# A quarter of the weight tiles' remainders on GpSimd in the mixing stages of a two-layer hybrid backbone

## The chip, the core and the metric

The kernel runs on one core of a Trainium2 chip. The metric is the device time of one launch in microseconds (us). Three runs of the kernel before gave a median of 2957.7 us. The engines are named as in the profile: PE is the matrix engine's matmul row (TensorE), PEld its weight load, DVE is VectorE, ACT is ScalarE, POOL is GpSimd, SP issues the DMAs. Each engine works through its own list of instructions in the order in which they stand, and waits at the first whose inputs or buffers are not ready.

## What is computed

Two layers over 256 latent and 256 context tokens of width 1024, in float32. Cut to what matters here:

```python
def layer(x, s, l):                       # x latent tokens, s context tokens, 256 of each
    x, s = ffn_sublayer(x, ...), ffn_sublayer(s, ...)        # SwiGLU, D_FF = 2816
    hx, hs = modulate(rms_norm(x)), modulate(rms_norm(s))
    cols = h @ w_in                                          # the wide projection of both streams
    ret = retention(cols[...])                               # 8 heads
    att = window_context_attention(cols[...])                # 8 heads
    rw = rwkv7(cols[...])                                    # 8 heads, forward and backward scan
    x = x + gate * ((g_ret * (ret @ w_ret) + g_att * (att @ w_att) + g_rw * (rw @ w_rwkv)) @ w_out)
    x = ffn_sublayer(x, ...)
```

In the second layer the mixing stage works out the latent tokens' results alone.

## The kernel before

**Products.** Every weight product is made of three matmuls in a rounded float32 format (`mm3`, L185 to L188): a value is split into a rounded part and the remainder. Lines 186, 187 and 188 multiply rounded weight by rounded activation, rounded weight by the activation's remainder, and the weight's remainder by the rounded activation. Where tokens are the output rows (`tokens`), the weight stands on the other side, and line 187 then reads the weight's remainder.

**Weight tiles.** `Weights.get` fetches the weights in the order of a plan, four 128x128 blocks (one tile of 128x512) at a time: SP issues a DMA into `raw` (8 buffers), ACT rounds it into `whi` (L114, 4 buffers), and DVE subtracts to give the remainder `wlo` (L115, 3 buffers). Three stages of a layer each have a `Weights` object: the first feed-forward, the mixing stage, the second feed-forward. The mixing stages' object is made with a fifth argument True, which is kept as `s.pool` and used nowhere.

**The mixing stage.** It runs over the words of `ORDER[l]`: `c` makes the columns of a pair of rwkv heads, `A` and `C` (`rw_front`, `rw_prep`) prepare its first and second 256 tokens, `B` and `D` (`rw_back`) finish them, `P` and `H` are retention, `kv`, `q`, `t` attention, `G` gates. At the end `branches` and `mix_out` multiply by the branch and output weights.

**The recurrence.** `rw_prep` ends in a triangular solve: a loop of 31 steps with two dependent GpSimd operations in each, a product (L999) and a sum (L1000), 62 operations in all. Its input `acc` comes by DMA through DRAM, and its result goes to `td` in DRAM and comes back as `z`. `rw_merge` then copies `z` on ACT (L1017), transposes it on DVE (L1014, L1018), and PE starts on it at L1026. There are 16 of these solves, for four pairs, two halves and two layers; below they are counted 0 to 15 in the order in which they run. Besides them POOL does only a few small copies (L921, L922, L934, L937) and 8 subtractions of 128x512 (L851).

**Order.** The order of instructions on every engine is not written out by hand. A scheduler at build time takes the program's order as priority and lets an instruction go when its own timing says that it is ready. A changed line so moves instructions on all engines.

Of the kernel before, what the change touches and what calls it, by code (L numbers as in the profile page):

```python
# [7 lines left out]
F32 = mybir.dt.float32  # L8
# [80 lines left out]
class Weights:  # L89
# [14 lines left out]
    def get(s, t, n=1):  # L104
        p = t // PB
        if p not in s.cur:
            nc = s.nc
            cols = min(PB, s.n - p * PB) * 128
            raw = s.mk([128, PB * 128], "raw", 8)[:, :cols]
            hi = s.mk([128, PB * 128], "whi", 4, F32R)[:, :cols]  # L110
            lo = s.mk([128, PB * 128], "wlo", 3, F32R)[:, :cols]
            o = p * PB * 16384
            s.last = nc.sync.dma_start(out=raw, in_=s.ap[o:o + 128 * cols].rearrange("(p c) -> p c", p=128)).ins
            nc.scalar.copy(hi, raw)  # L114
            nc.vector.tensor_sub(lo, raw, hi.bitcast(F32))  # L115
            s.cur = {q: v for q, v in s.cur.items() if q == p - 1}
            s.cur[p] = (hi, lo)
        hi, lo = s.cur[p]
        c = (t % PB) * 128
        return hi[:, c:c + 128 * n], lo[:, c:c + 128 * n]  # L120
# [1232 lines left out]
```

## Time and profile before

| | |
|---|---|
| median of three runs | 2957.7 us (2949.77 to 2957.78) |
| the profiled execution | 2949.03 us, span 2947.2 us |
| mean granted clock of PE | 0.965 of full speed |
| busy: PE, DVE, ACT, POOL | 96%, 68%, 43%, 13% of the span |
| mixing stages, both layers | 405 to 1310 us and 2060 to 2750 us of the span |

Busy shares are averages over the span. A busy PE is not a PE at its peak: at half the granted clock the same matmul takes longer and counts as busy.

### The profile page before, as it was taken

Reading aid. Unit: us, or ns where it says so; the run is one execution under the profiler, and the core shown is the slowest. Engines: PE = TensorE matmul, PEld = TensorE weight load, DVE = VectorE, ACT = ScalarE, POOL = GpSimd, SP = SyncE. Lnnn points to the kernel's source line nnn. Section 1 sums busy time; section 2 is a strip of 40 time slices with the busy share of each in tenths; the row PEclk is TensorE's granted clock in tenths of the full one; section 3 lists DMA queues with packets and bytes.
Section 4 is the critical chain, followed back from the end, with each engine's and each line's share of the span. In section 5 each row is a group of like instructions: output and inputs, shape, how many; then the busy total and the mean of one; then the engine's idle time right before and its main releaser. Section 6 shows DMA issues by size and latency. Waiting matters only on the chain.

```text
span 2947.2 us, 47745 instructions
## 1 busy us (share of the span) xinstructions
PE 2821.4 (96%) x17081; PEld 2413.6 (82%) x17081; DVE 1991.8 (68%) x4561; ACT 1261.4 (43%) x2776; POOL 372.5 (13%) x1068
## 2 busy tenths in 40 slices
PE   8999999899999999899999999999989899989999
PEld 7888888777887787688888888888878788878999
DVE  7977668776685765467756567455777677667655
ACT  3322245545445544333222332223556565655544
POOL 0000000622032201000000000000033344330000
PEclk9999999878999999899999999999999899999999
DMA  7655544222332145434635345344333244246554
GB/s 267 232 189 184 163 122 131 83 67 58 118 101 86 53 129 188 136 111 155 202 129 160 122 132 170 127 147 138 116 112 110 65 120 120 69 128 198 164 182 158
DMA packets 259726, 400.98 MB, mean 136 GB/s; under 512 B 78752, under 2 KB 96288, under 8 KB 259488
## 3 DMA queue, kind: packets, MB, share of 16 engines
q1 hardware_dynamic: 259488, 397.93, 43.1%
q8 instruction: 134, 2.20, 0.3%
q14 instruction: 104, 0.85, 0.1%
HBM read 368.33 MB, written 25.82 MB: 134 GB/s over the span
## 4 chain that ended last, share of the span: by engine, by line
PE 79%; POOL 7%; DVE 5%; DMA 4%; issue 2%; ACT 2%; SPq 1%; POOLq 0%; DVEq 0%; ACTq 0%
PE ps_mm L186 21%; PE ps_mm L187 20%; PE ps_mm L188 20%; POOL cst L1000 3%; POOL cst L999 3%; PE ps_rf L971 2%; PE ps_mm L364 1%; PE ps_po L774 1%; PE ps_rx L1075 1%; PE ps_rx L1068 1%; PE ps_rx L364 1%; PE ps_po L559 1%; DMA z<-td 1%; DVE wlo L115 1%; DMA td<-cst 1%
## 5 line engine op out<-in xcount | busy, mean ns | idle before, releaser
L186 PE MATMUL ps_mm<-hall,whi 128*128 128x512 f32 (+1 forms) x2320 | 843.2, 364 | 6.4 <-ACT kv L711 2.7
L114 ACT CAST whi<-raw 128x512 fp32r<-128x512 f32 x954 | 568.4, 617 | 655.1 <-PE ps_mm L187 429.7
L188 PE MATMUL ps_mm<-hall,wlo 128*128 128x512 f32 (+1 forms) x2320 | 839.7, 363 | 1.0 <-DVE wlo L115 1.0
L187 PE MATMUL ps_mm<-hall,whi 128*128 128x512 f32 (+1 forms) x2320 | 839.0, 362 | 0.0
L115 DVE TENSOR_TENSOR wlo<-raw,whi 128x512 fp32r<-128x512 f32 x954 | 645.8, 689 | 230.0 <-issue 106.8
L186 PEld LDWEIGHTS ps_mm<-hall,whi 128*128 128x128 f32 x2320 | 441.0, 190 | 78.5 <-ACT kv L711 3.1
L188 PEld LDWEIGHTS ps_mm<-hall,wlo 128*128 128x128 f32 x2320 | 439.9, 190 | 72.1 <-DVE wlo L115 2.4
L187 PEld LDWEIGHTS ps_mm<-hall,whi 128*128 128x128 f32 x2320 | 440.6, 190 | 70.5 <-issue 0.3
L186 PE MATMUL ps_mm<-hid,whi 128*128 128x512 f32 (+1 forms) x737 | 260.6, 354 | 0.0
L187 PE MATMUL ps_mm<-hid,whi 128*128 128x512 f32 (+1 forms) x737 | 259.9, 354 | 0.0
L188 PE MATMUL ps_mm<-hid,wlo 128*128 128x512 f32 (+1 forms) x737 | 257.4, 354 | 0.0
L999 POOL TENSOR_TENSOR cst<-acc,cst 128x60 f32<-128x60 f32 (+24 forms) x496 | 171.9, 347 | 599.7 <-DMA acc<-ad__10854 71.0
L851 POOL TENSOR_TENSOR ll<-lora,lh 128x512 fp32r<-128x512 f32 x8 | 10.2, 1278 | 1380.9 <-DMA raw<-w1b 949.7
L1000 POOL TENSOR_TENSOR cst<-cst 128x60 f32<-128x60 f32 (+24 forms) x496 | 172.7, 348 | 37.8
L236 DVE SCALAR_TENSOR_TENSOR ft<-m,cd 128x1024 bf16<-128x1024 f32 x136 | 162.8, 1219 | 6.0 <-DMA m<-ada 6.0
L237 DVE SCALAR_TENSOR_TENSOR m<-m,cd 128x1024 f32<-128x1024 f32 x136 | 165.3, 1220 | 0.7
L373 DVE SCALAR_TENSOR_TENSOR x<-ps_mm,cst,x 128x256 f32<-128x256 f32 x136 | 61.0, 480 | 146.6 <-PE ps_mm L188 146.3
L187 PEld LDWEIGHTS ps_mm<-hid,whi 128*128 128x128 f32 x737 | 139.1, 189 | 19.5
L186 PEld LDWEIGHTS ps_mm<-hid,whi 128*128 128x128 f32 x737 | 139.0, 189 | 19.5
L188 PEld LDWEIGHTS ps_mm<-hid,wlo 128*128 128x128 f32 x737 | 138.5, 189 | 19.4
L401 DVE TENSOR_TENSOR ft<-ft,ps_mm 128x512 f32<-128x512 f32 (+1 forms) x80 | 49.6, 620 | 126.1 <-PE ps_mm L188 120.7
L210 ACT CAST hid<-ft 128x512 fp32r<-128x512 f32 (+1 forms) x88 | 49.9, 568 | 192.5 <-DVE ft L401 192.4
(338 smaller groups left out, 4560.8 us busy)
## 6 DMA issues: line engine op xcount, KB each, us to landing
m<-ada SPq DMA_DIRECT2D x136, 512.0 KB, 4.3
raw<-w0b SPq DMA_DIRECT2D x214, 256.0 KB, 2.9
raw<-w1b SPq DMA_DIRECT2D x211, 256.0 KB, 3.0
raw<-w0a SPq DMA_DIRECT2D x132, 256.0 KB, 3.0
raw<-w0c SPq DMA_DIRECT2D x132, 256.0 KB, 3.1
raw<-w1a SPq DMA_DIRECT2D x132, 256.0 KB, 3.0
raw<-w1c SPq DMA_DIRECT2D x132, 256.0 KB, 3.9
gd<-ft SPq DMA_DIRECT2D x24, 256.0 KB, 2.6
```

The source lines that it names most:

```text
L114: nc.scalar.copy(hi, raw)
L115: nc.vector.tensor_sub(lo, raw, hi.bitcast(F32))
L186: PE.matmul(o, w[0], h[0], start=start, stop=False)
L187: PE.matmul(o, w[0], h[1], start=False, stop=False)
L188: PE.matmul(o, w[1], h[0], start=False, stop=stop)
L236: V.scalar_tensor_tensor(junk, raw, 1.0, st["cond"][0], ALU.mult, ALU.mult, accum_out=md[:, kt, 0:1])
L237: V.scalar_tensor_tensor(raw, raw, 1.0, st["cond"][1], ALU.mult, ALU.mult, accum_out=md[:, kt, 1:2])
L364: PE.matmul(o[:, p], w[k, j][q], hl(H[k], p)[0], start=(k == 0 and q == 0 and p.start == c.start), stop=False)
L373: V.scalar_tensor_tensor(xs[n][:, CS[s]], o[:, CS[s]], gate[:, n, s:s + 1], xs[n][:, CS[s]], ALU.mult, ALU.add)
L971: PE.matmul(ov[:, q, 0:n], kb[d][hs, q].rearrange("p a t -> p (a t)"), ar[d][hs, q].rearrange("p a t -> p (a t)")[:, 0:n], start=True, sto ...
L999: G.tensor_tensor(w, acc[j // 16][:, j % 16, j + 1:32].unsqueeze(1).to_broadcast([128, m, n]), tt[:, 0:m, j:j + 1].to_broadcast([128, m, n ...
L1000: G.tensor_tensor(tt[:, 0:m, j + 1:32], tt[:, 0:m, j + 1:32], w, ALU.add)
```

## The change

One line. In the mixing stages every fourth weight tile (those with number 3, 7, 11, ... of the plan) has its remainder taken on GpSimd:

```diff
@@ -112,7 +112,7 @@
             o = p * PB * 16384
             s.last = nc.sync.dma_start(out=raw, in_=s.ap[o:o + 128 * cols].rearrange("(p c) -> p c", p=128)).ins
             nc.scalar.copy(hi, raw)
-            nc.vector.tensor_sub(lo, raw, hi.bitcast(F32))
+            (nc.gpsimd if s.pool and p % 4 == 3 else nc.vector).tensor_sub(lo, raw, hi.bitcast(F32))
             s.cur = {q: v for q, v in s.cur.items() if q == p - 1}
             s.cur[p] = (hi, lo)
         hi, lo = s.cur[p]
```

104 of the 954 remainders change engine (some tiles are fetched twice, by `tokens`). The set of instructions is otherwise the same, but their order is not: 26 of the 104 now stand inside a recurrence. In recurrence 13 (second layer, its input is `acc_23514`) POOL's list read, before:

```order
L999 TENSOR_TENSOR cst_63<-acc_23514,cst_63 128x69
L1000 TENSOR_TENSOR cst_63<-cst_63 128x3x23
L999 TENSOR_TENSOR cst_63<-acc_23514,cst_63 128x66
L1000 TENSOR_TENSOR cst_63<-cst_63 128x3x22
L999 TENSOR_TENSOR cst_63<-acc_23514,cst_63 128x63
```

and now:

```order
L999 TENSOR_TENSOR cst_63<-acc_23514,cst_63 128x69
L1000 TENSOR_TENSOR cst_63<-cst_63 128x3x23
L999 TENSOR_TENSOR cst_63<-acc_23514,cst_63 128x66
L115 TENSOR_TENSOR wlo_24534<-raw_24532,whi_24533 128x512
L1000 TENSOR_TENSOR cst_63<-cst_63 128x3x22
L999 TENSOR_TENSOR cst_63<-acc_23514,cst_63 128x63
```

A tile's subtraction stands between two dependent steps; a second one (`wlo_25020`) follows 18 operations later.

The copies of `z` of the same recurrence, on ACT in the second layer. Before, they stood right behind the first two activations of the next half's preparation (L908, L909):

```order
L908 ACTIVATE rt_25091<-ps_rf_25093,cst_63 128x256
L909 ACTIVATE rt_25092<-ps_rf_25093,cst_63 128x256
L1017 COPY tg_19027<-z_24814 32x8x32 x2
L772 COPY aT_24336<-ps_ap_24335 128x512
L1077 COPY ve_24611<-ps_rx_24640 64x128
```

Now they stand further back, behind L939 of that preparation, and `aT_24336` has gone ahead of them:

```order
L918 ACTIVATE rt_25117<-rt_25108 128x512
L919 ACTIVATE rt_25118<-rt_25108 128x512
L765 ACTIVATE ae_24352,cst_63<-ps_sc_24351,cst_63 128x512
L939 ACTIVATE rt_25131<-rt_25092,cst_63 128x512
L1017 COPY tg_19027<-z_24814 32x8x32
L777 ACTIVATE cst_63<-cst_63 128x4
L1077 COPY ve_24611<-ps_rx_24662 64x128
```

DVE's transposes of that `z` moved back by as much.

The third place is recurrence 4 (first layer, its input is `acc_7793`), on POOL. Before, no tile stood there. Now one stands behind the first 17 operations of the recurrence:

```order
L1000 TENSOR_TENSOR cst_63<-cst_63 128x2x24
L999 TENSOR_TENSOR cst_63<-acc_7793,cst_63 128x69
L115 TENSOR_TENSOR wlo_8526<-raw_8524,whi_8525 128x512
L1000 TENSOR_TENSOR cst_63<-cst_63 128x3x23
L999 TENSOR_TENSOR cst_63<-acc_7793,cst_63 128x66
```

The tile `wlo_8526` has to wait for that recurrence's input and steps, and PE for the tile.

## Rows read from the trace of the kernel before

**Rows 1.** The page: busy time by engine, and the chain of waits by engine.

```profile
PE 2821.4 (96%) x17081; PEld 2413.6 (82%) x17081; DVE 1991.8 (68%) x4561; ACT 1261.4 (43%) x2776; POOL 372.5 (13%) x1068
...
PE 79%; POOL 7%; DVE 5%; DMA 4%; issue 2%; ACT 2%; SPq 1%; POOLq 0%; DVEq 0%; ACTq 0%
```

**Rows 2.** Busy time by stretch: span, PE, PEld, DVE, ACT, POOL, clock, DMA.

```profile
405.00:1130.00 725.00, 691.38 (x4467) 582.20 (x4466) 501.37 (x1338) 368.11 (x906) 175.20 (x532) 0.94 0.31 91
1130.00:1310.00 180.00, 167.65 (x854) 133.01 (x853) 104.93 (x214) 66.62 (x130) 0.00 (x0) 0.95 0.50 167
...
2060.00:2640.00 580.00, 535.20 (x4087) 469.74 (x4085) 423.27 (x1121) 333.73 (x817) 197.11 (x532) 0.95 0.37 105
2640.00:2750.00 110.00, 100.42 (x815) 95.07 (x815) 81.97 (x207) 53.69 (x125) 0.00 (x0) 0.92 0.59 184
```

**Rows 3.** The page's costliest groups: busy us, mean ns of one, idle before.

```profile
L115 DVE TENSOR_TENSOR wlo<-raw,whi 128x512 fp32r<-128x512 f32 x954 | 645.8, 689 | 230.0 <-issue 106.8
...
L999 POOL TENSOR_TENSOR cst<-acc,cst 128x60 f32<-128x60 f32 (+24 forms) x496 | 171.9, 347 | 599.7 <-DMA acc<-ad__10854 71.0
L851 POOL TENSOR_TENSOR ll<-lora,lh 128x512 fp32r<-128x512 f32 x8 | 10.2, 1278 | 1380.9 <-DMA raw<-w1b 949.7
```

**Rows 4.** Timeline beside L851: start, duration, idle before in brackets.

```profile
2072.86 1.28 POOL L851 TENSOR_TENSOR ll<-lora,lh 128x512 fp32r<-128x512 f32 x1 [949.69 <-DMA raw<-w1b]
2073.23 1.19 DVE L303 SCALAR_TENSOR_TENSOR hall<-ft,cst,hall 128x256 fp32r<-128x256 f32 x1 [0.84 <-ACT hall L302]
...
2074.41 0.47 DVE L303 SCALAR_TENSOR_TENSOR hall<-ft,cst,hall 128x256 fp32r<-128x256 f32 x1
```

**Rows 5.** Timeline of POOL, recurrence 13, early operations and the last.

```profile
2470.66 0.24 POOL L999 TENSOR_TENSOR cst<-acc,cst 128x30 f32<-128x30 f32 x1
2470.97 0.56 POOL L1000 TENSOR_TENSOR cst<-cst 128x30 f32<-128x30 f32 x1
...
2499.00 0.21 POOL L1000 TENSOR_TENSOR cst<-cst 128x8 f32<-128x8 f32 x1
```

**Rows 6.** Waits of the whole span: total us, times, longest.

```profile
ACT tg L1017 <- DMA z<-td: 57.9, 18, 6.7
...
DVE tg L1018 <- DMA z<-td: 35.1, 10, 5.1
```

**Rows 7.** Timeline of ACT and PE at the merge of recurrence 13.

```profile
2499.26 0.47 ACT L909 ACTIVATE rt<-ps_rf,cst 128x256 f32<-128x256 f32 x1
...
2505.68 0.83 ACT L1017 COPY tg<-z 32x256 f32<-32x256 f32 x2 [5.96 <-DMA z<-td]
...
2507.18 1.97 PE L774 MATMUL ps_po<-kv,aT 128*128 128x64 f32 x8 [5.24 <-ACT aT L772]
...
2513.60 0.80 ACT L939 ACTIVATE rt<-rt,cst 128x512 f32<-128x512 f32 x1
```

**Rows 8.** Timeline of ACT and PE at the merge of recurrence 15.

```profile
2639.89 0.40 ACT L1017 COPY tg<-z 32x256 f32<-32x256 f32 x1 [4.15 <-DMA z<-td]
...
2640.63 0.49 PE L1079 MATMUL ps_rx<-ve,kbT 128*128 128x128 f32 x2 [3.79 <-ACT ve L1077]
```

**Rows 9.** Stretches behind those two stops, columns as in rows 2.

```profile
2504.00:2511.00 7.00, 3.82 (x16) 3.30 (x17) 3.23 (x10) 4.30 (x12) 0.00 (x0) 0.54 0.34 80
2641.00:2652.00 11.00, 11.00 (x102) 9.95 (x101) 5.62 (x22) 4.52 (x15) 0.00 (x0) 0.53 0.39 121
```

**Rows 10.** Timeline: first use of wlo_8526 on PE, start of recurrence 4.

```profile
842.07 0.28 PE L187 MATMUL ps_mm<-wlo,hall 128*128 128x256 f32 x1
...
846.33 0.41 POOL L999 TENSOR_TENSOR cst<-acc,cst 128x31 f32<-128x31 f32 x1 [55.89 <-DMA acc<-ad__7790]
```

**Rows 11.** Timeline of PE, two neighbouring full-width matmuls of a weight product.

```profile
1221.63 0.40 PE L188 MATMUL ps_mm<-hall,wlo 128*128 128x512 f32 x1
1221.87 0.40 PE L186 MATMUL ps_mm<-hall,whi 128*128 128x512 f32 x1
```

## The prediction

> **What bounds the kernel now.** First the page's busy times: PE is busy for 96% of the span, DVE for 68%, POOL for 13% [rows 1]. Then the stretches, because the change acts in the mixing stages alone: there PE still works for 692 of 725 us, 168 of 180, 535 of 580 and 100 of 110, so it stands idle for about 100 us in all, while DVE is busy for 58 to 75% and nowhere full [rows 2]. The granted clock of PE is 0.92 to 0.95 there [rows 2], so some of PE's busy time is at the lower of its two levels (1.2 instead of 2.4 GHz). What can be won or lost are these 100 us and the time at the lower level; PE's work itself doesn't change. Third the chain of waits: 79% of it runs over PE, 7% over POOL, 5% over DVE [rows 1]. POOL's 7% are recurrences: eleven of the sixteen (0, 1, 4, 5 in the first layer, 8, 9, 10, 12, 13, 14, 15 in the second) lie on that chain, some in part. So the engine that looks idle is on the path, and the one that is relieved hardly is. Fourth the waits: ACT stands 57.9 us, in 18 waits, in front of L1017 until `z` has come back from DRAM, and DVE 35.1 us in front of L1018 [rows 6]. All that stands behind those copies on ACT and DVE waits along.
>
> **What is removed from DVE, and what it gets back.** 104 subtractions leave DVE, at 0.689 us each [rows 3]: 71.7 us. They come to POOL. The trace of before has no remainder there, but L851 is the same operation in the same shape and types (128x512 float32 to the rounded format), at 1.278 us [rows 3]: 133 us more for POOL, which has far more idle time than that. DVE doesn't keep its 71.7 us. While an L851 ran, DVE's L303 took 1.19 us, where the next one of the same shape took 0.47 [rows 4]: a DVE operation with two inputs in SBUF stood still for 0.72 us. Beside the eight L851 this happened four times (0.7 to 1.1 us each, 0.9 on average); the other four times DVE had an operation on PSUM or nothing. Half of 104 by 0.9 is 47 us, which leaves DVE a relief of some 24 us over 1,600. The bounds are 0 and 24 us. I take 3, near the low end, since DVE is 5% of the chain.
>
> The Trainium skill, "SBUF — State Buffer", section "SBUF: two separate sides", says that GpSimd and a VectorE operation with two SBUF inputs share a port pair as an exclusive lock for a whole instruction. Rows 4 agree in kind: 0.72 us of 1.28 were lost there. By that rule alone the relief would shrink to nothing, which is the second rival below.
>
> **The same stop the other way shortens the recurrences.** A step of a recurrence takes 0.24 us beside a quiet DVE and 0.56 where a DVE operation with two SBUF inputs runs [rows 5]. Laid side by side in time, 177 of the 992 steps (the first and last of them in one recurrence are in [rows 5]) meet an L115 and take 0.54 us on average, and those that meet no DVE operation 0.27. With a quarter fewer L115 on DVE some 44 steps lose 0.26 us each, 11.5 us in sixteen recurrences, 8 us in the eleven on the chain. Bounds 0 and 11.5; I take 8.
>
> **Tiles inside recurrences.** 26 of the 104 stand between the first and the last step of a recurrence, as `wlo_24534` does. They lengthen it by 1.28 us each [rows 3]. 20 of them are in recurrences that lie on the chain: 2, 0, 3, 1 in the first layer's four and 3, 3, 0, 2, 2, 3, 1 in the second's seven. Unhidden that is 25.6 us. What hides it: the order of after puts L1017 and L1014 further back. In recurrence 13 ACT before had finished L909 at 2499.7 and then stood for 5.96 us; now the copy stands behind L939, which in before ended at 2514.4, 8.7 us after `z` was there [rows 7]. Two tiles make `z` 2.6 us later, so it is there before ACT comes. The merges of 0, 8 and 15 moved back in the same way, by more than their tiles cost; together with 13 they hold 8 of the 20 tiles. For the other 12 the shift is small or nothing, and I charge them in full: 12 by 1.28 is 15.4 us. If a recurrence comes late, what waits is ACT at L1017, behind it the rounding of the next weight tiles (L114), and then PE.
>
> **Stops that go.** Behind the copy in recurrence 13 stood `aT`, and PE waited 5.24 us for it [rows 7]; in recurrence 15 it waited 3.79 us in the same way [rows 8]. Behind each stop PE ran at 0.53 to 0.54 of its clock, so at the lower level for nearly all of a stretch of 7 and of 11 us [rows 9]; half of what it does there is lost, some 8.5 us in all. The merge copies no longer stand in front of those operations. I count both waits as gone, 9.0 us, and half of the clock's loss, 4 us: 13. Bounds: 0, if the same wait turns up one instruction later, and 17.5.
>
> **Places where the order gets worse.** `wlo_8526` stands behind 17 steps of recurrence 4. By the old times PE wants it at 842.1 and the recurrence begins at 846.3 [rows 10]; 17 steps and the tile itself end at about 854.5, so PE would wait over 12 us. But the order has moved on PE too: what the recurrence's input is made of comes 6.6 us of PE's work earlier and the tile's first use 5.6 later, 12.2 together, which leaves next to nothing; for a tile that POOL begins late because DVE holds it up I take 1.5. Bounds 0 and 12.4. In the first layer, B0's chain of small matmuls had 48 full-width weight matmuls among them and now has 6; 42 by 0.24 us [rows 11] are 10 us of cover that is used up earlier. PE was at a low clock there anyhow; between 0 and 10 I take 4.
>
> **Edits at nothing.** The other 78 tiles stand between recurrences, most of them with POOL idle. At the old times POOL ends nearly all of them 1.5 us or more before PE's first use, also at the end of both layers, where the order on ACT and PE is nearly the old one; what covers them are the three `wlo` buffers and PE's own three matmuls a block. Without that cover each costs at most its extra 0.6 us, 46 us in all.
>
> **The sum.** 15.4 - 8 - 13 - 3 + 1.5 + 4 = -3.1 us, against the profiled execution's 2949.0 (its span of 2947.2 and 1.8 around it): 2945.9. The three runs' median, 2957.7, is 8.7 above that execution, so the forecast for a median is **2954.6 us**. A measurement of this kernel tells about 0.3%, 8.9 us, from no change: the forecast lies within it.
>
> **The rivals.** *The recurrences decide (slower).* POOL's list is worked off in order, so a tile in a recurrence waits for its `whi` and a free `wlo` buffer, which PE gives back, and with it the rest of the solve. If the copies' shift covers nothing, all 20 tiles count (25.6) and no stop goes: 25.6 - 8 - 3 + 1.5 + 4 = +20, 2977.8. It decides once `z` lands later than ACT reaches L1017 at most merges. For it: ACT already waits there at most merges [rows 6]. Against it: the new order.
>
> *The port decides (slower).* If every moved tile stops DVE for its full 1.28 us, DVE loses 133 us and is given 71.7: 62 us worse. A quarter of it on the path gives some 16 in place of -3: +16, 2974. For it: rows 4. Against it: half of the L851 stopped nothing. The Trainium skill, "Perfetto Trace Analysis", section "Optimizing Scalar/DVE Operations", warns that shifting work between these two engines might not help because of that port.
>
> *The stops were the loss (faster).* If the later copies take away the stops at all merges, the tiles cost 5 us instead of 15.4, the clock comes back in full (17.5 instead of 13) and B0 loses nothing: 5 - 8 - 17.5 - 3 + 1.5 = -22, 2935.7. For it: 57.9 us of ACT's waits [rows 6]. Against it: only recurrences 13 and 15 stop PE for long.
>
> That nothing changes (all hidden) is inside the forecast.
>
> **Chances.** Forecast 0.46, spread about 9 us to either side: 0.08 of it faster, 0.04 slower, 0.34 within 0.3%. Faster rival 0.30; recurrences 0.15; port 0.09. So faster 0.38, same 0.34, slower 0.28. The range takes in the faster and the slower rival's numbers: 2933 to 2980. The forecast's own is 2945 to 2964.
>
> **What would show it.** Right: L115 on POOL at 1.28 us, more where DVE holds the port; ACT's wait at L1017 well under 57.9 us; PE's stops before L774 at recurrence 13 and L1079 at recurrence 15 gone; recurrences with two or three tiles 1 to 4 us longer, those without shorter; DVE's L303 and scans at over 1 us beside L115 on POOL. Wrong: PE waiting for `wlo` more than a few us, ACT's L1017 wait as long as before, or a lower clock in stretches where it was full. The clock's low stretches are worth tens of us and need not stay where they are: that is the likeliest way for this to miss.

## The result and the profile after

The changed kernel took **2983.3 us** (median of 4 runs, 2981.0 to 2986.5), the kernel before 2953.7 beside it: ratio 1.0095, 95% interval 1.0079 to 1.0112. It was timed twice more: 2968.8 us, 1.0045 [1.0028, 1.0062], and 2975.9 us, 1.0053 [1.0035, 1.0071]. So the change makes this kernel slower, by 0.45 to 0.95%, 13 to 28 us; the forecast was 2954.6, and the range ended at 2980.

The page of the changed kernel, busy times and the chain of waits by engine [rows 1]:

```profile
PE 2845.0 (95%) x17081; PEld 2426.9 (81%) x17081; DVE 1973.9 (66%) x4457; ACT 1265.7 (42%) x2776; POOL 502.6 (17%) x1172
...
PE 44%; POOL 4%; DVE 3%; DMA 1%; issue 1%; ACT 1%; SPq 0%; POOLq 0%; DVEq 0%
```

The span grew from 2947.2 to 2981.1 us. The chain's shares add up to 54% of the span here and to 100% in [rows 1], so they can't be held against each other. PE's busy time, for as many matmuls, grew by 23.6 us, and the granted clock fell from 0.965 to 0.955; the rest of the span, in which PE stands idle, grew from 125.8 to 136.1. The stretches of the mixing stages, columns as in [rows 2]:

```profile
405.00:1130.00 725.00, 680.82 (x4328) 567.57 (x4327) 487.30 (x1266) 362.38 (x880) 219.89 (x535) 0.92 0.31 89
1130.00:1310.00 180.00, 165.21 (x855) 129.70 (x854) 103.72 (x208) 65.58 (x141) 26.79 (x50) 0.94 0.48 157
2060.00:2640.00 580.00, 544.00 (x3909) 477.66 (x3908) 410.38 (x1090) 323.06 (x779) 212.21 (x507) 0.91 0.37 106
2640.00:2750.00 110.00, 98.44 (x858) 88.91 (x857) 71.33 (x185) 57.22 (x145) 35.13 (x72) 0.95 0.56 171
```

In the two long ones the granted clock fell from 0.94 and 0.95 to 0.92 and 0.91. Between 2060 and 2640 us PE is even busier than before and yet does fewer matmuls (3909 for 4087). The stretches are fixed in time and the changed kernel runs late by then (recurrence 8 ends at 2227.8 us for 2194.0), so they don't hold quite the same work. The costliest groups, columns as in [rows 3]:

```profile
L115 DVE TENSOR_TENSOR wlo<-raw,whi 128x512 fp32r<-128x512 f32 x850 | 593.6, 712 | 94.9 <-ACT whi L114 77.8
L115 POOL TENSOR_TENSOR wlo<-raw,whi 128x512 fp32r<-128x512 f32 x104 | 142.8, 1373 | 678.2 <-ACT whi L114 536.2
...
L999 POOL TENSOR_TENSOR cst<-acc,cst 128x60 f32<-128x60 f32 (+24 forms) x496 | 167.1, 337 | 278.4 <-DMA acc<-ad__9657 37.6
L851 POOL TENSOR_TENSOR ll<-lora,lh 128x512 fp32r<-128x512 f32 x8 | 10.7, 1342 | 1204.4 <-ACT lh L850 781.9
```

The 104 take 1.373 us each on POOL, against the 1.278 that was taken from L851. DVE lost 71.7 us of work and is only 17.9 us less busy. The waits for `z` [rows 6]:

```profile
ACT tg L1017 <- DMA z<-td: 46.1, 23, 5.5
DVE rb L1014 <- DMA z<-td: 27.1, 8, 7.9
...
PE ps_rx L1123 <- DVE rb L1120: 16.5, 4, 4.8
...
DVE tg L1018 <- DMA z<-td: 13.7, 6, 4.8
```

L1017 waits less than before, as forecast (46.1 for 57.9), and so does L1018 (13.7 for 35.1). Below, the sum of L1017, L1014 and L1018 is "the waits for z": 115.6 us before, 86.9 after. Every run also has a "length of the recurrences": from the start of the first L999 to the end of the 31st L1000, read from POOL's timeline and summed over the sixteen. It grew from 431.2 to 463.6 us.

### The profile page after: what moved, and what is told of

Read it like the earlier page. It is cut to its first block, busy times and chain, and to the rows that moved or that the text cites. A ratio compares the mean times of both kernels' runs of the same rounds, so it can differ in the third digit from the quotient of the medians.

```text
span 2981.1 us, 47795 instructions
## 1 busy us (share of the span) xinstructions
PE 2845.0 (95%) x17081; PEld 2426.9 (81%) x17081; DVE 1973.9 (66%) x4457; ACT 1265.7 (42%) x2776; POOL 502.6 (17%) x1172
## 4 chain that ended last, share of the span: by engine, by line
PE 44%; POOL 4%; DVE 3%; DMA 1%; issue 1%; ACT 1%; SPq 0%; POOLq 0%; DVEq 0%
PE ps_mm L186 12%; PE ps_mm L188 12%; PE ps_mm L187 12%; POOL cst L999 2%; POOL cst L1000 2%; PE ps_rf L971 1%; PE ps_mm L364 1%; PE ps_rx L364 1%; DVE wlo L115 0%; POOL wlo L115 0%; DMA z<-td 0%; PE ps_rx L1068 0%; PE ps_rx L1075 0%; PE ps_po L774 0%; PE ps_mm L369 0%
## 5 line engine op out<-in xcount | busy, mean ns | idle before, releaser
L188 PE MATMUL ps_mm<-hall,wlo 128*128 128x512 f32 (+1 forms) x2320 | 843.6, 364 | 3.2 <-DVE wlo L115 3.1
L187 PE MATMUL ps_mm<-hall,whi 128*128 128x512 f32 (+1 forms) x2320 | 840.3, 362 | 0.5 <-DVE hall L211 0.5
L115 DVE TENSOR_TENSOR wlo<-raw,whi 128x512 fp32r<-128x512 f32 x850 | 593.6, 712 | 94.9 <-ACT whi L114 77.8
L188 PEld LDWEIGHTS ps_mm<-hall,wlo 128*128 128x128 f32 x2320 | 440.5, 190 | 76.6 <-DVE wlo L115 4.9
L187 PEld LDWEIGHTS ps_mm<-hall,whi 128*128 128x128 f32 x2320 | 441.3, 190 | 72.0 <-DVE hall L211 0.9
L187 PE MATMUL ps_mm<-hid,whi 128*128 128x512 f32 (+1 forms) x737 | 260.0, 354 | 0.0
L188 PE MATMUL ps_mm<-hid,wlo 128*128 128x512 f32 (+1 forms) x737 | 257.4, 354 | 0.0
L115 POOL TENSOR_TENSOR wlo<-raw,whi 128x512 fp32r<-128x512 f32 x104 | 142.8, 1373 | 678.2 <-ACT whi L114 536.2
L999 POOL TENSOR_TENSOR cst<-acc,cst 128x60 f32<-128x60 f32 (+24 forms) x496 | 167.1, 337 | 278.4 <-DMA acc<-ad__9657 37.6
L851 POOL TENSOR_TENSOR ll<-lora,lh 128x512 fp32r<-128x512 f32 x8 | 10.7, 1342 | 1204.4 <-ACT lh L850 781.9
L1000 POOL TENSOR_TENSOR cst<-cst 128x60 f32<-128x60 f32 (+24 forms) x496 | 167.2, 337 | 36.6
L187 PEld LDWEIGHTS ps_mm<-hid,whi 128*128 128x128 f32 x737 | 139.1, 189 | 19.5
L188 PEld LDWEIGHTS ps_mm<-hid,wlo 128*128 128x128 f32 x737 | 138.5, 189 | 19.5
```

The source lines that it names most:

```text
L115: (nc.gpsimd if s.pool and p % 4 == 3 else nc.vector).tensor_sub(lo, raw, hi.bitcast(F32))
L187: PE.matmul(o, w[0], h[1], start=False, stop=False)
L188: PE.matmul(o, w[1], h[0], start=False, stop=stop)
L999: G.tensor_tensor(w, acc[j // 16][:, j % 16, j + 1:32].unsqueeze(1).to_broadcast([128, m, n]), tt[:, 0:m, j:j + 1].to_broadcast([128, m, n ...
L1000: G.tensor_tensor(tt[:, 0:m, j + 1:32], tt[:, 0:m, j + 1:32], w, ALU.add)
```

## The experiments

An edit here changes the order on every engine, since the scheduler lays all instructions out anew. To tell the order from the engine, most runs hold an order fixed: the program is laid out once, and laid out again with each instruction bound to follow the one that stood before it on its engine.

```diff
+    first, traced = build(arrays, False)
+    order = [i.name for i in first.all_instructions() if i.name in traced]
+    nc, _ = build(arrays, True, {n: j for j, n in enumerate(order)})
...
+            for i in sorted((i for i in traced if i.name in rank), key=lambda i: rank[i.name]):
+                if i.engine in last:
+                    tc.add_manual_dep(i, last[i.engine].name, NOSYNC, reason="order")
+                last[i.engine] = i
```

"Order of before" and "new order" (that of the changed kernel) are meant so. Ratios are to the kernel before on the same chip, with 95% intervals; us are the ratio times 2958, a median of before. "PE idle" is the span less PE's busy time in the one execution of each kernel that was profiled.

| Order | On POOL | median us | ratio | us | recurrences | waits for z | PE idle |
|---|---|---|---|---|---|---|---|
| of before | none (e3) | 2953.7 | 0.9985 [0.9971, 0.9998] | -4 | 433.3 | 115.4 | 120.5 |
| of before | all 104 (e1) | 2977.6 | 1.0059 [1.0046, 1.0072] | +17.5 | 458.6 | 158.0 | 140.8 |
| of before | 79 outside recurrences (e5) | 2957.7 | 0.9999 [0.9990, 1.0009] | 0 | 430.9 | 117.2 | 123.4 |
| of before | 25 inside (e6) | 2972.4 | 1.0044 [1.0028, 1.0060] | +13 | 460.2 | 139.7 | 137.4 |
| new | none (e2) | 2954.8 | 0.9993 [0.9981, 1.0006] | -2 | 441.4 | 66.6 | 131.2 |
| new | all 104 (e13) | 2966.9 | 1.0035 [1.0017, 1.0052] | +10 | 465.1 | 90.7 | 139.0 |
| new | 78 outside (e11) | 2961.4 | 1.0010 [0.9996, 1.0025] | +3 | 444.9 | 64.0 | 139.4 |
| new | 26 inside (e12) | 2961.8 | 1.0014 [0.9996, 1.0031] | +4 | 475.6 | 83.1 | 129.9 |
| its own | 104 others (e4) | 2975.3 | 1.0056 [1.0040, 1.0073] | +16.5 | 471.0 | 67.9 | 138.5 |

The waits for z compare runs of one order only: every kernel of another order than that of before has shorter ones, e4 and the changed kernel too, which are slower.

### Order or engine: e1 to e4

e1 puts the 104 on POOL in the order of before, e2 puts them back on DVE in the new order, e3 writes the order of before out and changes nothing, e4 takes other tiles in an order of its own. e4's line against that of the changed kernel:

```diff
-(nc.gpsimd if s.pool and p % 4 == 3 else nc.vector).tensor_sub(lo, raw, hi.bitcast(F32))
+(nc.gpsimd if s.pool and p % 4 == 1 else nc.vector).tensor_sub(lo, raw, hi.bitcast(F32))
```

> Every engine runs its instructions in the order of the kernel before; only the 104 remainders sit on GpSimd, at the place that their turn in that order gives them. Theory 'order' (the loss of 30 us lies in the new order of the other engines): the time of before within 0.3%, 2945 to 2962 us. Theory 'recurrences' (tiles between the steps delay the merges): slower by 15 to 30 us, 2969 to 2984, with longer waits of L1017 and L1018 for z than the 93 us of before. Theory 'port' (each GpSimd subtraction keeps VectorE out): slower by 10 to 20 us spread over the mixing stages, 2964 to 2974. By the prediction's terms that don't hang on a new order (+15.4 - 8 - 3 + 1.5) it would be some 6 us slower, 2960.

> Every engine runs its instructions in the order of the changed kernel, but the 104 remainders are back on VectorE at the place of their turn. Theory 'order': as slow as the changed kernel, 2975 to 2990 us, with the same PE gaps at the single-block products of the first mixing stage. Theories 'recurrences' and 'port': the loss goes, 2945 to 2962 us.

> The kernel before, with the order that it has anyway written out for every engine. All theories: the time of before within 0.3%, 2945 to 2962 us; any more would mean that writing the order out costs something by itself, and the other two fixed orders would have to be read against this.

> As many remainders go to GpSimd, but those with p % 4 == 1 in place of 3, and the scheduler orders it anew. Theory 'order': the time is a new draw, anywhere from 2940 to 2995 us, with its loss or gain at other places than 580 to 616 us. Theories 'recurrences' and 'port': the load on GpSimd and its tiles between the steps are the same, so 2975 to 2990 us again.

My first theory was that the new order was the loss. It fell: the new order with DVE doing the work costs nothing (e2), the old one with POOL doing it costs 17.5 us (e1). e4 took 2975.3 us, 1.0056 [1.0040, 1.0073], as the other theories expected (the first had allowed anything from 2940 to 2995). e3 shows that a written order has no price (-4 us).

e2 also shows what became of the stops that were to go. Timeline of PE in e2, idle time before in brackets:

```profile
2467.80 0.55 PE L186 MATMUL ps_mm<-whi,hall 128*128 128x256 f32 x1 [7.39 <-DVE rr_v L799]
...
2709.34 0.66 PE L1123 MATMUL ps_rx<-cst,rb 64*128 64x64 f32 x4 [5.11 <-DVE rb L1120]
```

The waits of 5.24 and 3.79 us in [rows 7, 8] are not there, but PE now stands 7.39 us before recurrence 13, and 5.11 us at the end of the layer, where it was 3.4. The first of these is e2's alone; the changed kernel has others (below).

### Inside or outside the recurrences: e5 to e8, e11, e12

In the order of e1, 25 remainders stand between the steps of a recurrence and 79 do not; in the new order 26 and 78. `STEP` lists those inside; e6, e11 and e12 differ from e5's line, shown against the changed kernel, in the test on `STEP` and in the order that is held.

```diff
-o = p * PB * 16384
+o = p * PB * 16384; s.pool and p % 4 == 3 and SEEN.append(p)
...
-(nc.gpsimd if s.pool and p % 4 == 3 else nc.vector).tensor_sub(lo, raw, hi.bitcast(F32))
+(nc.gpsimd if s.pool and MOVED[0] and p % 4 == 3 and len(SEEN) - 1 not in STEP else nc.vector).tensor_sub(lo, raw, hi.bitcast(F32))
```

> Order of before on every engine; on GpSimd only the 79 remainders that stand outside the 16 recurrences, the 25 between their steps stay on VectorE. Theory 'late tiles' (products wait for a remainder that stands between two steps of a recurrence, and the clock falls behind the stop): the time of before within 0.3%, 2946 to 2963 us. Theory 'longer recurrences' (25 x 1.3 us between the steps make the merges late): the same, 2946 to 2963. Theory 'port' (each subtraction on GpSimd slows VectorE): 79/104 of the 18 us remain, 2965 to 2975.

> Order of before; on GpSimd only the 25 remainders that stand between steps of the recurrences. 'Late tiles' and 'longer recurrences': all of the 18 us, 2968 to 2980, with products waiting for remainders of GpSimd as in the run with all 104. 'Port': 25/104 of it, 2955 to 2965.

In this order the 79 outside cost nothing, and the 25 inside cost 13 of the 17.5 us. "Port" as the main cause fell with this. The way on which a tile inside can cost shows at recurrence 4. Timeline of POOL, DVE and PE in the kernel before, the end of the recurrence and its merge:

```profile
874.19 0.22 POOL L1000 TENSOR_TENSOR cst<-cst 128x8 f32<-128x8 f32 x1
...
881.03 0.43 DVE L1014 STREAM_TRANSPOSE rb<-z 32x256 f32<-32x256 f32 x1 [1.59 <-DMA z<-td]
...
881.52 0.69 PE L1026 MATMUL ps_rx<-rb,cst 32*32 32x32 f32 x16 [0.48 <-DVE rb L1014]
```

The same with ACT in e6, where two remainders stand in this recurrence:

```profile
881.85 0.21 POOL L1000 TENSOR_TENSOR cst<-cst 128x8 f32<-128x8 f32 x1
...
888.70 0.41 ACT L1017 COPY tg<-z 32x256 f32<-32x256 f32 x1 [4.66 <-DMA z<-td]
888.70 0.43 DVE L1014 STREAM_TRANSPOSE rb<-z 32x256 f32<-32x256 f32 x1 [5.00 <-DMA z<-td]
...
889.18 1.05 PE L1026 MATMUL ps_rx<-rb,cst 32*32 32x32 f32 x16 [4.81 <-DVE rb L1014]
```

And PE in e5, where none stands in it:

```profile
882.51 1.06 PE L1026 MATMUL ps_rx<-rb,cst 32*32 32x32 f32 x16 [4.40 <-DVE rb L1014]
```

The last step comes 7.7 us later, 4.3 of them because the recurrence itself began later. Both copies of `z` wait longer, with all that stands behind them on ACT and DVE; PE waits 4.81 us for 0.48, and its next 16 matmuls take 1.05 us for 0.69, at half the granted clock (0.50 for 1.00). But the same order waits here without a tile too: 4.40 us in e5, 3.42 in e3. So this merge shows the way, and not the price of the two tiles. That is in the sums: against e3, which has the same order and nothing on POOL, the recurrences of e6 are 27 us longer, the waits for z 24 us and PE's idle time 17 us. Over the whole span the waits of e6:

```profile
ACT tg L1017 <- DMA z<-td: 78.0, 22, 10.7
DVE tg L1018 <- DMA z<-td: 40.7, 11, 9.0
DVE rb L1014 <- DMA z<-td: 21.0, 5, 7.2
...
PE ps_mm L188 <- POOL wlo L115: 6.5, 3, 3.3
PE ps_rf L971 <- POOL ar L937: 4.1, 1, 4.1
```

There is a second way, the late tile. Timeline of POOL and PE in e1, recurrence 8:

```profile
2185.64 0.38 POOL L999 TENSOR_TENSOR cst<-acc,cst 128x72 f32<-128x72 f32 x1
2185.98 1.44 POOL L115 TENSOR_TENSOR wlo<-raw,whi 128x512 fp32r<-128x512 f32 x1
...
2187.47 0.54 PE L188 MATMUL ps_mm<-hall,wlo 128*128 128x512 f32 x1 [2.37 <-POOL wlo L115]
```

The tile stood behind the steps, and PE waited 2.37 us for it. In e6 such waits add up to 6.5 us at L188 and 2.8 at L187, so they can be a good part of its 17 us; the changed kernel has none. To separate the two, e7 and e8 leave every remainder on DVE and let POOL do an idle subtraction behind it, 104 or only the 79 outside.

```diff
-nc.vector.tensor_sub(lo, raw, hi.bitcast(F32))
+sub = nc.vector.tensor_sub(lo, raw, hi.bitcast(F32)).ins.name; s.pool and p % 4 == 3 and MOVED[0] and EXTRA.update({nc.gpsimd.tensor_sub(raw.bitcast(F32R), raw, raw).ins.name: sub})
```

> Order of before, and VectorE keeps all remainders; GpSimd does 104 subtractions of the same size (raw minus raw into raw, used by nobody) behind them in the same places. No product can wait for a remainder on GpSimd. 'Late tiles': the time of before within 0.3%, 2946 to 2963 us. 'Longer recurrences': the merges are as late as with the real ones, 2966 to 2980. 'Port': VectorE has all its work and is slowed as well, 2968 to 2990, with a mean of L115 on VectorE above 0.71 us.

> As the run before this, with only the 79 subtractions outside the recurrences. 'Late tiles' and 'longer recurrences': the time of before within 0.3%, 2946 to 2963 us. 'Port': 2963 to 2985 us.

e7: 3004.6 us, 1.0149 [1.0133, 1.0165]; recurrences 468.8 us, waits for z 162.6. No product can wait for POOL there and the loss is larger than any theory expected, so late tiles alone don't make it. e7 isn't quite the same load, since an idle subtraction first waits for DVE to be done with `raw`: some 14 of its 37.6 us more in the recurrences are such waits. How e6's loss divides between the two ways stays open. e8: 2964.6 us, 1.0020 [1.0008, 1.0033]: 79 subtractions that relieve nobody cost 6 us, at the low end of what "port" expected. The group of L115 in e8 on both engines:

```profile
L115 DVE TENSOR_TENSOR wlo<-raw,whi 128x512 fp32r<-128x512 f32 x954 | 646.9, 698 | 28.1 <-ACT whi L114 10.5 <-issue 6.3 <-PE ps_mm L188 2.7
...
L115 POOL TENSOR_TENSOR raw<-raw 128x512 fp32r<-128x512 f32 x79 | 94.4, 1195 | 748.6 <-DVE wlo L115 455.6 <-issue 126.7 <-ACT whi L114 66.2
```

DVE is busy for 2002.6 us there and for 1979.7 in e3, which has the same order and the same work on DVE (1981.2 and 1981.6 in e9 and e10, which have it too): 0.29 us a subtraction. I take that to be the port's price, and that with the real remainders (e5, 0 us) DVE's relief pays it back. The Trainium skill, "SBUF — State Buffer", section "SBUF: two separate sides", calls the shared port pair an exclusive lock; the stops agree with that, but 0.29 us of 1.195 is what a subtraction took from DVE on average.

> Order of the changed kernel; the 26 remainders that stand between steps there go back to VectorE, the other 78 stay on GpSimd. Theories 'longer recurrences' and 'late tiles': the whole loss goes, the time of before within 0.3%, 2948 to 2966 us. If the new order and GpSimd's load only lose together, whichever tiles are moved: 2970 to 2985 us.

> Order of the changed kernel; only the 26 remainders between steps stay on GpSimd. 'Longer recurrences' and 'late tiles': as slow as the changed kernel or more, 2975 to 2992 us. Otherwise 2950 to 2966 us.

In the new order neither half costs what can be measured. e12's runs spread from 2955.8 to 2981.1 us, and both theories had expected 2975 and more from it. So that the tiles inside are what costs is shown for the order of before alone; here PE's idle time is no longer with them (129.9 us for e2's 131.2). (In e12's profiled execution, its slowest, a remainder in recurrence 13 itself waited 9.6 us; that is in its 475.6.) Since the changed kernel had cost 28 us, the two halves seemed to cost more together.

### Are the halves additive: e13, e14, e17

> The changed kernel with the order that it has anyway written out for every engine, all 104 remainders on GpSimd. If the two halves cost more together than apart: as slow as the changed kernel, 2978 to 2992 us. If the changed kernel loses by something other than order and engine (which buffers its tiles share): 2955 to 2970 us, the sum of the halves (0.10% + 0.14%).

> The changed kernel once more, on the same chip as the run before: 0.8 to 1.1% over before in either case.

> The changed kernel a third time. If the second occasion was the typical one, 0.3 to 0.6% over before; if the first, 0.8 to 1.1%; if it differs by chip, anything between.

e13 costs 10 us [5, 15]. Against e2 the halves are +5 and +6, and all 104 +12, each to within some 6 us: no sign that they cost more together. e14 and e17, the change itself, came at half of the first ratio: what was off was the first timing. Its page has PE at 2845.0 us busy; e14's page, the same kernel on another occasion:

```profile
PE 2831.8 (95%) x17081; PEld 2415.2 (81%) x17081; DVE 1973.7 (66%) x4457; ACT 1265.0 (43%) x2776; POOL 503.5 (17%) x1172
```

13.2 us less PE time for the same matmuls in the same order, and no less idle time (span 2973.0, so 141.2 for 136.1): the clock. Laid side by side, matmul by matmul, most of it sits in two places. Two stretches of the execution profiled at the first timing, columns as in [rows 2]:

```profile
1001.07:1018.47 17.40, 17.40 (x98) 15.04 (x96) 4.93 (x11) 7.13 (x20) 0.00 (x0) 0.51 0.12 27
2561.00:2581.39 20.39, 20.39 (x95) 18.39 (x94) 6.18 (x18) 6.40 (x21) 0.00 (x0) 0.50 0.06 14
```

The same 98 and 95 matmuls in e14:

```profile
1001.66:1011.36 9.70, 9.70 (x98) 8.46 (x96) 4.83 (x11) 6.63 (x19) 0.00 (x0) 1.00 0.13 30
2557.28:2568.38 11.10, 11.10 (x95) 10.00 (x95) 5.78 (x18) 6.19 (x21) 0.00 (x0) 1.00 0.04 7
```

PE never stands idle in them, and yet the clock is at its lower level in one execution and full in the other: 7.7 and 9.3 us. Just before, PE was as busy in both: 9.5 of 10 us ahead of the first, all 7 us ahead of the second. Of the seven profiled executions in the new order, three lost the whole of the first (the first timing's, e11, e12) and four the second (the first timing's, e12, e13, e17); e2 and e14 lost neither. So times in this order can differ by steps of this size. All four runs of the first occasion had granted clocks of 0.954 to 0.956, the twelve of e14 and e17 of 0.958 to 0.966. What decides whether the clock falls there stays open, and with one profiled execution of each kernel so does how much of e13's 12 us it is.

### Length of the recurrences alone: e9 and e10

No remainder moves. At the 25 places (`MORE`) the step's product is repeated, into the same tile; e10 has 8 in place of 4.

```diff
-G.tensor_tensor(w, acc[j // 16][:, j % 16, j + 1:32].unsqueeze(1).to_broadcast([128, m, n]), tt[:, 0:m, j:j + 1].to_broadcast([128, m, n]), ALU.mult)
+step = [G.tensor_tensor(w, acc[j // 16][:, j % 16, j + 1:32].unsqueeze(1).to_broadcast([128, m, n]), tt[:, 0:m, j:j + 1].to_broadcast([128, m, n]), ALU.mult).ins.name for _ in range(1 + 4 * MOVED[0] * MORE[REC[0]].count(j + 1))]; EXTRA.update({x: step[0] for x in step[1:]}); REC[0] += j == 30
```

> Order of before, all remainders on VectorE. At the 25 places where remainders stood between steps, GpSimd repeats the step's product (L999) four more times, 100 x 0.35 = 35 us of recurrence in all, about what the 25 remainders took there with their waits (33.8 + 4.0 us). Theory 'longer recurrences': as slow as with the 25 remainders, 2966 to 2982 us. Theory 'late tiles': no product waits for GpSimd, the time of before within 0.3%, 2948 to 2966 us.

> The same with eight repeats at each of the 25 places, some 70 us of recurrence. 'Longer recurrences': at least as much again, 2985 to 3015 us, since what slack the merges had is used up by the first 35. 'Late tiles': 2948 to 2968 us.

e9: 3002.8 us, 1.0138 [1.0119, 1.0156], +41 us. e10: 3038.5 us, 1.0262 [1.0244, 1.0280], +77 us. Both are above what was expected. The recurrences were 39 and 76 us longer: in the order of before every us showed in the time, from the first on. There is no slack that has to be used up. Not all of it is waiting: in the profiled executions PE's idle time grew by 32 and 66 us against e3's, and the rest is busy time at a lower clock (0.949 and 0.948 for 0.958). The waits of e10:

```profile
ACT tg L1017 <- DMA z<-td: 122.5, 18, 15.4
DVE tg L1018 <- DMA z<-td: 68.3, 13, 14.3
DVE rb L1014 <- DMA z<-td: 40.8, 5, 13.7
PE ps_rf L971 <- POOL ar L937: 11.6, 2, 9.6
```

For z 231.6 us, against 171.3 in e9 and 115.6 before. e9 was slower than "as the 25 remainders" had let me expect: they lengthen the recurrences by 29 us and cost 13.

### What DVE's relief is worth: e15 and e16

```diff
-nc.vector.tensor_sub(lo, raw, hi.bitcast(F32))
+lo = hi if s.pool and MOVED[0] and p % 4 == 3 and len(SEEN) - 1 in STEP else (LO.append((s.pool and p % 4 == 3 and len(SEEN) - 1 in STEP, nc.vector.tensor_sub(lo, raw, hi.bitcast(F32)).ins.name)), lo)[1]
```

> Order of before; the 25 remainders that stand between steps of the recurrences are left out, and their products take the rounded weights in place of the remainder. What this saves is VectorE's time there alone (17 us). If that relief is what makes 25 moved remainders (13 us) cheaper than 100 extra steps (41 us, 31 for the 29 us by which the 25 lengthen the recurrences): 12 to 20 us faster, ratio 0.993 to 0.996. If VectorE's time is worth nothing there: within 0.3%.

> Order of before; all 104 remainders are left out in the same way. This is the most that taking them off VectorE can bring in this order. If VectorE's relief counts only inside the recurrences: as the run before, 12 to 22 us faster. If it counts nowhere: within 0.3%. If it counts everywhere: 25 us and more.

e15: 2947.5 us, 0.9967 [0.9954, 0.9980], -10 us; the recurrences are 9.5 us shorter (421.7). e16: 2940.7 us, 0.9949 [0.9931, 0.9967], -15 us, recurrences 420.9. So 72 us of DVE's work are worth some 15 [10, 20], and 10 of these come with the 25 inside, where the shorter recurrences account for them. This does not explain why e6 costs less than its length, as I had thought: the shorter steps are already in the 460.2 us.

### The other direction: e18

If POOL's list decides, taking work out of the recurrences must bring something. e18 has the order of before; the small copies go to ACT, L851 to DVE.

```diff
-        G.tensor_sub(ll, lw, lh.bitcast(F32))
+        (V if MOVED[0] else G).tensor_sub(ll, lw, lh.bitcast(F32))
...
-                G.tensor_copy(ar[d][:, :, 0, 63:64], kkc[:, :, 63:64])
+                (A.copy if MOVED[0] else G.tensor_copy)(ar[d][:, :, 0, 63:64], kkc[:, :, 63:64])
```

> Order of before, all remainders on VectorE, and GpSimd keeps its steps only: the 64 small copies (L921, L922, L934, L937) go to ScalarE and the 8 subtractions of L851 to VectorE, at the places of their turn. In before, 28 of the copies (8.1 us) and 3 of the subtractions (3.9 us) stood between steps. If every us of recurrence shows in the time: 8 to 14 us faster, ratio 0.995 to 0.9975. If only late weight tiles matter: within 0.3%. If ScalarE's or VectorE's extra work weighs more: slower.

**2935.3 us** beside 2956.8, 0.9920 [0.9906, 0.9935]: 24 us faster, the best of all these kernels and more than expected. The recurrences are 8.2 us shorter (423.0), the waits for z hardly changed. The group of L999 in e18:

```profile
L999 POOL TENSOR_TENSOR cst<-acc,cst 128x60 f32<-128x60 f32 (+24 forms) x496 | 173.4, 350 | 2238.4 <-DMA acc<-ad__19665 1039.8 <-DMA acc<-ad__3958 515.0 <-DMA acc<-ad__7790 110.8
```

POOL has nothing but the steps left. What the expectation overlooked is the other side of a list worked off in order: the copies also waited behind steps, and PE for them. The wait of L971 for `ar` (L937) was 1.6 us before, 4.1 in e6 and 11.6 in e10; in e18 there is none. That this makes up the other 15 us is argued, not shown. The clock is a rival: e18's six runs had 0.963 to 0.970, the eleven of before beside them 0.959 to 0.964, and by the medians of both (0.9675 for 0.960) PE's 2820 us of work take some 22 us less, an estimate. In its profiled execution PE's idle time is much as in e3 (118.1 us for 120.5), and its busy time is 19.3 us less.

## Why the prediction was wrong

Two steps of the sum failed: the gain from stops that go (forecast -9 with B0's +4, measured -2), and the price of the tiles on POOL (forecast 15.4 - 8 - 3 + 1.5 = 5.9, measured 12 from e2 to e13). Together they are the 13 us between the sum, -3.1, and e13's +10. What the first timing shows beyond that is the clock.

**Tiles inside recurrences: a step that failed.** I let the new order's later copies cover 8 of 20 tiles and charged 12, at 1.28 us. At recurrence 13, the case worked out there, the timeline of ACT and PE after:

```profile
2539.18 0.81 ACT L939 ACTIVATE rt<-rt,cst 128x512 f32<-128x512 f32 x1
2542.28 0.40 ACT L1017 COPY tg<-z 32x256 f32<-32x256 f32 x1 [2.29 <-DMA z<-td]
...
2543.12 1.22 PE L1079 MATMUL ps_rx<-ve,kbT 128*128 128x128 f32 x4 [2.59 <-ACT ve L1077]
```

The copy does stand behind L939, and yet it waits 2.29 us for `z`, and PE waits 2.59 us behind it. In e2, the same order with the tiles on DVE, the copy of ACT and the transpose of DVE there:

```profile
2516.40 0.43 DVE L1014 STREAM_TRANSPOSE rb<-z 32x256 f32<-32x256 f32 x1 [0.58 <-DMA z<-td]
...
2518.03 0.39 ACT L1017 COPY tg<-z 32x256 f32<-32x256 f32 x1
```

ACT comes 1.6 us after DVE has got `z`, and doesn't wait. So the cover was about 1.6 us and not 8.7, and two tiles of 1.36 us used it up. The 8.7 came from [rows 7], where L939 had itself stood behind the copy's wait of 5.96 us; without that wait it would have ended some 2.8 us after `z` was there. At the other merges that I counted as covered (0, 8, 15) ACT waits 3.69, 4.43 and 2.72 us for `z` in the changed kernel.

The lengthening was forecast well: 26 by 1.28 less 11.5 makes 21.8 us in the sixteen recurrences, and it is 22 to 24 (463.6 and 465.1 against e2's 441.4). What it costs in the new order is not settled. My terms for the tiles on POOL make 5.9 us and 12 were measured, but the halves, +6 inside and +5 outside, don't tell which term was too small. PE's idle time grows by only 8 us from e2 to e13, though the waits for z grow by 24: unlike in the order of before, most of the lengthening doesn't reach PE there.

**Stops that go: the step that failed most clearly.** -13, with +4 for B0's chain (never tried by itself), makes -9 for the new order alone. e2 gave -2 [-6, +2]. Both stops did go; others as long came elsewhere. PE's stops of more than 3 us, from 400 us of the span on, add up to 24.7 us before, 30.8 in e2 and 37.3 in the changed kernel. (The 8.5 us of clock counted both stretches whole; PE was busy for 14.8 of their 18 us, which gives 7.4.) Reading two stops that vanish, without those that appear, takes half of an exchange for a gain.

**What was right.** DVE's relief: 71.7 us out and 47 back was forecast, 53.8 came back. Worth little: e5 gives 0 where I took -3. The shorter steps: 11.5 us forecast in the sixteen recurrences, of which 8 counted; e15 is 9.5 shorter and 10 us faster. The tiles outside at nothing: so in e5; in the new order e11 has +5 against e2, just within the noise. The 1.5 us for `wlo_8526` were nothing: in the changed kernel PE waits for no remainder of POOL. (The 854.5 us in that step leave the tile itself out, 1.28 us.) Of the signs that I named for being wrong, only the lower clock came.

**The rivals.** "The recurrences decide" (all tiles count, no stop goes) gave 2977.8, at a chance of 0.15, and is the nearest in number: +20 forecast, +10 to +28 measured. Its condition, `z` landing after ACT gets to L1017, held: ACT waits there at all sixteen merges after, 23 times. In the order of before it is what e6, e9 and e10 show; in the new order it isn't shown, the two stops did go, and part of its number is the clock, so it was in part lucky. "The port decides" fell with e5 and e8: 6 us for 79 subtractions. So the warning of the Trainium skill, "Perfetto Trace Analysis", section "Optimizing Scalar/DVE Operations", that moving work between these two might not help, came true here, in the order of before, by way of POOL's queue more than of the port. "The stops were the loss" fell with e2.

**The sum, as measured.** New order -2; the 78 outside +5 and the 26 inside +6 against that (each within some 6 us); together +10 (e13), and up to +28 with the clock of the first occasion, 17 us of it, against e14, in two stretches of the execution that was profiled. No term of mine held that, though the last sentence named it.

Open: why 25 remainders add 24 us to the waits for z and 100 repeated steps at the same places 56, though the recurrences grow by 29 and 39; which of the tiles cost in the new order; and what lowers the clock at the two places.

## What to carry to other kernels

An engine that is busy for 13% of the time can still be the one with no slack: what counts is whether its list holds a serial chain that others wait for in order. Before giving it work, ask where in that list the work will stand; in the order of before the same subtraction cost nothing between the chains and half a us inside them, and the gain (24 us) came from taking work off the idle-looking engine. An old time on a list that is worked off in order contains the waits ahead of it: take them out before using it as cover. Where a scheduler lays everything out anew, fix the order and change the engine, then the other way round, before believing either.

## What the runs showed of the hardware

The same instructions in the same order don't get the same clock: the two stretches of e14 and of the first timing above, 0.50 and 0.51 of full speed in one execution and 1.00 in the other, with PE busy throughout. The page of e3, which is the kernel before with its order written out:

```profile
PE 2836.9 (96%) x17081; PEld 2426.2 (82%) x17081; DVE 1979.7 (67%) x4561; ACT 1245.7 (42%) x2776; POOL 374.1 (13%) x1068
```

PE is 15.5 us longer busy there than in [rows 1] with less idle time (120.5 us of 2957.4 for 125.8 of 2947.2), at a granted clock of 0.958 for 0.965. Single executions of one kernel lie up to 18 us apart (2948.3 to 2966.1 in 23 runs of before), so one profile against another tells less than the medians; the length of the recurrences (433.3 and 431.2) and the waits for z (115.4 and 115.6) repeat far better.
